# A Hymba-style layer on one Trainium2 core: the second feed-forward's operand blocks moved by 384 bytes, and the ends of its down projections multiplied in token halves

## The chip, the core and the metric

The program runs on one core of one Trainium2 chip. The core has a matrix engine (TensorE, "PE" in the profile, with its weight loads listed apart as "PEld"), a vector engine (DVE), a scalar engine (ACT), GpSimd (POOL) and a queue engine (SP) that issues the loads from HBM. A time is the device time of one launch in microseconds (us). Three runs of the kernel before gave 1117.93, 1118.01 and 1118.09 us. The profile is one more execution, looked at instruction by instruction.

## The reference

One layer over 512 latent tokens and 256 context tokens of width 1024, float32. All three stages run over the latent tokens, and the first two also over the context. The change touches the third stage alone:

```python
def swiglu(h, w1, w3, w2):
    return (jax.nn.silu(h @ w1) * (h @ w3)) @ w2

def ffn_sublayer(h_in, shift, scale, gate, norm_w, w1, w3, w2):
    h = modulate(rms_norm(h_in, norm_w), shift, scale)
    return h_in + 0.5 * gate * swiglu(h, w1, w3, w2)
...
    x = ffn_sublayer(x, mx[0], mx[1], mx[2], norm1_w, ffn1_w1, ffn1_w3, ffn1_w2)
...
    x = x + mx[5] * token_mix(proj, k_all, v_all, rope, q_a_norm_w, w_uq, q_norm_w,
                              v_norm_w, w_s, b_s, w_out)
...
    x = ffn_sublayer(x, mx[6], mx[7], mx[8], norm3_w, ffn2_w1, ffn2_w3, ffn2_w2)
```

With 512 tokens, `w1` and `w3` are 1024 x 2816 and `w2` is 2816 x 1024. The hidden width of 2816 is 22 tiles of 128 columns.

## The kernel before, in words

**Products in three parts.** Activations lie transposed: 128 features on the partitions, tokens along the free axis. Every float32 operand is kept as two tiles, a rounded part (`h`) and the rest (`l`). `mm3` (line 165) makes a product of three matmuls: weights-high with tokens-high, weights-high with tokens-low, weights-low with tokens-high. In the profile's names, `one<-t1h,oph` is a matmul that streams tile `t1h` (the tokens, the moving operand) through the loaded weights `oph` into PSUM bank `one`. Each matmul has its own weight load of 128 x 128.

**The split weights.** Raw weights come from HBM in tiles `raw` or `block`. ACT rounds 512 columns of them into `oph`, and DVE writes the remainder into `opl` (`Stream.split`). There are five such pairs (`OPS = 5`), used in turn.

**The second feed-forward.** Its tokens come as four blocks of 4 feature tiles x 256 tokens: `B11`, `B21` (first 256 tokens), `B12`, `B22` (last 256). The first four hidden tiles (`NPLAIN2 = 4`) are multiplied plainly, 256 tokens at a time (`plain_mm`, lines 168 to 170 in the profile where the scheduler sets the order); part of them take weights from tiles `w0`, `w1` and from the places of `T3` and `T4`. The other 18 hidden tiles go through a Strassen-Winograd scheme (`class Winograd`): seven products each instead of eight, with the blocks `B11`, `B21`, `B22` and the sums `T1` to `T4`. Such a product (`prod`) is 4 feature tiles x 3 matmuls of 128 weights x 256 tokens, so a hidden tile takes 7 x 12 = 84 matmuls. GpSimd and DVE make the sums of weight blocks, ACT and DVE split them and evacuate the banks.

**The down projections.** The 22 hidden tiles are multiplied with `w2` in six chunks, `CHUNKS2 = [4, 4, 4, 4, 2, 4]`. After the last hidden tile of a chunk, `down_flow` (line 746) runs over the 8 output tiles; for each it adds up `n` hidden tiles with `n` x 3 matmuls of 128 weights x 512 tokens into one bank `mm`. Its moving operands are `gh` and `gl`, and its weights are again `oph` and `opl`. The first five chunks take this way (called from `after2`, line 2059); the sixth goes through `down`, at the very end, whose last output tile is done in two halves of 256 tokens.

**What sets the order.** From the Winograd part's start to the fifth down projection the order on every engine is the order written (`nc.ordered = "all"`; all these instructions carry line 59, which is the helper that pins them). What follows is ordered by the scheduler. Line numbers are those of the kernel before.

**Where the tiles lie.** Tiles are taken from pools that grow from both ends of the on-chip memory (SBUF). A tile's start in its partition, in bytes, modulo 512, in the built program:

```
tiles                                       before   after
oph, opl (split weights, all five pairs)       384     384
gh, gl (second feed-forward)                   384     384
B12                                            384     384
B11, B21, B22, T1, T2, T3, T4 (each h and l)   448      64
w0, w1 (each h and l), hfA, squares, rstd      448      64
pth, ptl (attention, moving)                   128     128
vv (attention values, weights)                 448     448
```

Slices of 128 weights and of 256 tokens start at multiples of 512 bytes behind these. "Distance" below is the moving operand's start minus the weights' start, modulo 512: 64 for a block with `oph` or `opl` before (448 - 384), 0 for `gh` or `gl` with `oph` or `opl`, 192 for `pth` with `vv` (128 - 448 + 512).

Of the kernel before, what the change touches and what calls it, by code (L numbers as in the profile page):

```python
# [9 lines left out]
F32 = mybir.dt.float32  # L10
# [7 lines left out]
P = 128  # L18
D = 1024
NK = D // P  # L20
# [11 lines left out]
CHUNKS2 = [4, 4, 4, 4, 2, 4]  # L32
# [132 lines left out]
def mm3(nc, out, lhs, rhs, first, last, more=False):  # L165
    lh, ll = lhs
    rh, rl = rhs
    nc.tensor.matmul(out, lh, rh, start=first, stop=False, skip_group_check=more)  # L168
    nc.tensor.matmul(out, lh, rl, start=False, stop=False, skip_group_check=more)  # L169
    nc.tensor.matmul(out, ll, rh, start=False, stop=last, skip_group_check=more)  # L170
# [3 lines left out]
def layer_kernel(ctx: ExitStack, tc: tile.TileContext, xT, wfirst, wst, wada, wuq, wkpe, cols, wrope, vnw, rope, out):  # L174
    nc = Core(tc)
# [24 lines left out]
    def mm():  # L200
        return ps.tile([P, 512], F32, tag="mm", bufs=4, name=f"mm_{nc.next_id()}")
# [10 lines left out]
    pairs = [[const.tile([P, NK, 2], F32, name=f"{n}{i}") for n in "sag"] for i in range(3)]  # L212
# [189 lines left out]
    def evac_lat(pt, dt, i):  # L402
        nc.vector.scalar_tensor_tensor(lat(x, dt), two(pt), mod_g[i][0][:, dt : dt + 1], lat(x, dt), ALU.mult, ALU.add)
# [286 lines left out]
    def span(t, g, n):  # L690
        if g == "lat":
            return two(t)[:, :, 0:256]
        if g == "ctx":
            return two(t)[:, :, 256:384]
        return t[:, g : g + n]
# [47 lines left out]
        for p in range(2 * n):  # L743
            flow.todo.append(lambda p=p: want(p))

    def down_flow(flow, f0, n, groups, evac, step=lambda dt: None):
        pairs, gone = [], 0
        for dt in range(NK):
            flow.slot(lambda: step(dt))
            while 4 * len(pairs) < dt * n + n:  # L750
                pairs.append(flow.take())
            pts = []
            for g, gn in groups:
                pts.append(mm())
                for fi in range(n):
                    q, o = divmod(dt * n + fi, 4)
                    c = slice(o * P, o * P + P)
                    gh, gl = gt[f0 + fi]
                    mm3(nc, pts[-1][:, :gn], [t[:, c] for t in pairs[q]], (span(gh, g, gn), span(gl, g, gn)), fi == 0, fi == n - 1)
            for (g, gn), pt in zip(groups[:-1], pts):  # L760
                evac(pt, dt, g, gn)
            def last(pt=pts[-1], dt=dt, g=groups[-1]):
                evac(pt, dt, *g)
                yield

            flow.pend = [last()]
            flow.spent = (dt * n + n) // 4 - gone
            gone += flow.spent

    starts1 = [sum(CHUNKS1[:i]) for i in range(len(CHUNKS1))]  # L770
    starts2 = [sum(CHUNKS2[:i]) for i in range(len(CHUNKS2))]
# [203 lines left out]
    def after1(flow, f):  # L975
        for ci in ends1(f):
            down_flow(flow, starts1[ci], CHUNKS1[ci], [GA, GB], lambda pt, dt, g, gn: evac_x(pt, dt, seg_of(g // 384), 0),
                      lambda dt: ada_step(2))
# [61 lines left out]
    flow = Flow(OPS)  # L1040
# [35 lines left out]
    for f in range(NFIRST, NPLAIN1):  # L1076
# [7 lines left out]
        for w in range(2):  # L1084
            pair = None
            for g in (1, 0) if last else (0, 1):
# [12 lines left out]
                for k in range(NK):  # L1099
                    c = slice(k % 4 * P, k % 4 * P + P)  # L1100
# [5 lines left out]
                if w == 1:  # L1106
# [3 lines left out]
                    def evac(f=f, pb=(pb[g, 0], pb[g, 1]), c=slice(384 * g, 384 * g + 384)):  # L1110
                        gh, gl = gt[f]
                        sl = gp.tile([P, 384], F32, tag="sl", bufs=1, name=f"sl_{nc.next_id()}")
                        nc.scalar.activation(sl, pb[0][:, :384], AF.Silu)
                        nc.vector.tensor_mul(sl, pb[1][:, :384], sl)
                        yield
                        g_split(sl, gh[:, c], gl[:, c])
# [57 lines left out]
    def last_mm(g, dt):  # L1174
        pt = mm()
        c = slice(384 * g, 384 * g + 384)
        for fi in range(lastn):
            q, o = divmod(dt * lastn + fi, 4)
            gh, gl = gt[lastf + fi]
            mm3(nc, pt[:, :384], [t[:, o * P : o * P + P] for t in lastp[q]], (gh[:, c], gl[:, c]), fi == 0, fi == lastn - 1)  # L1180
        return pt
# [35 lines left out]
    pt = None  # L1217
    for dt in range(NK):
# [5 lines left out]
        pt = last_mm(0, dt)  # L1224
# [4 lines left out]
    def in_want(i, w):  # L1229
        if w == 0:  # L1230
            inw[i].append(st.half(wst, U_IN + i))
        src = inw[i][0][:, w * 512 : w * 512 + 512]
        inw[i].append(homes[2] if i == 2 and w else st.pair())
        hi, lo = inw[i][-1]
        nc.scalar.copy(hi, src)
        return lambda: nc.vector.tensor_sub(lo, src, hi.bitcast(F32))

    TILES = (0, 1, 2, 1, 2, 1, 1, 0)
    for dt in range(NK):
        w = in_want(dt - 5, 0) if dt > 4 else None  # L1240
# [10 lines left out]
        pt = last_mm(1, dt)  # L1251
# [367 lines left out]
    heads, pes, pts, sms, ols = {}, {}, {}, {}, {}  # L1619
# [231 lines left out]
    with right():  # L1851
        hap = hactx.enter_context(tc.tile_pool(name="hap", bufs=1))

    def block(pool, name):
        return tuple(pool.tile([P, 4, 256], F32R, bufs=1, name=f"{name}{p}") for p in "hl")

    B11, B21 = block(hap, "b11"), block(hap, "b21")
    hbctx = ExitStack()
    with right():
        hbp = hbctx.enter_context(tc.tile_pool(name="hbp", bufs=1))  # L1860
# [134 lines left out]
    def ends2(f):  # L1995
        return [ci for ci in range(len(CHUNKS2) - 1) if starts2[ci] + CHUNKS2[ci] == f]
# [33 lines left out]
    flow = Flow(OPS)  # L2030
# [27 lines left out]

    def after2(flow, f):
        for ci in ends2(f):  # L2060
            down_flow(flow, starts2[ci], CHUNKS2[ci], [(0, 512)], lambda pt, dt, g, gn: evac_lat(pt, dt, 2))

    nc.ordered = "all"
    wino.run(flow, NPLAIN2, after2, splits=splits)
    nc.ordered = False
    lastu = {}
# [104 lines left out]
```

## Time and profile before

| what | value |
|---|---|
| median of three runs | 1118.01 us |
| the profiled execution's own time | 1118.25 us |
| its span, first to last instruction | 1116.5 us |
| granted TensorE clock over the span | 1.000 |
| matmuls / weight loads | 7208 / 7208 |
| DVE, ACT, POOL busy | 80%, 48%, 28% of the span |
| last down projection's start to the end of the span | from about 1088 us to 1116.5 us |

A matmul's duration in the profile is modelled and longer than the time after which the next one starts, since matmuls are pipelined. What a matmul costs is the distance between two starts. So the views of use are the timeline (start times of single instructions), and windows laid exactly around a stretch of equal matmuls, whose length divided by their number is the cost of one.

### The profile page before, as it was taken

To read this page: it belongs to the slowest core of one execution; us is meant where nothing else is said; L and a number is where in the kernel's file an instruction comes from. 1 tells how busy PE (TensorE), PEld (TensorE's weight loads), DVE (VectorE), ACT (ScalarE), POOL (GpSimd) and SP (SyncE) were. 2 spreads that over 40 slices of the span, in tenths; PEclk is the share of its full clock that TensorE was granted. 3 is DMA by queue.
4 is the path that set the end of the run, shared out by engine and by line. 5 is a ranking of instruction groups with operands and counts; after the bars stand their busy time and mean duration, and the time that the engine had idled before them with its cause. 6 is when DMAs were issued, how large, how long until landed. Compare 5 with 4: busy or idle time off the path is not lost.

```text
span 1116.5 us, 18983 instructions
## 1 busy us (share of the span) xinstructions
PE 1111.0 (100%) x7208; PEld 1062.8 (95%) x7208; DVE 888.9 (80%) x1638; ACT 538.6 (48%) x1110; POOL 310.8 (28%) x268
## 2 busy tenths in 40 slices
PE   9999999999999999999999999999999999999998
PEld 7899999999999999999988889999999989898997
DVE  5779898888888789867756899978887869686884
ACT  6545412431444214444745559985554535353451
POOL 0002303312233023300018427750014435161330
PEclk9999999999999999999999999999999999999999
DMA  9721353344333665322243111003121422233302
GB/s 359 266 69 45 131 163 123 113 137 147 124 114 143 235 196 187 116 63 74 86 148 95 60 38 40 20 20 123 68 97 59 149 75 104 90 110 113 114 1 95
DMA packets 35675, 125.91 MB, mean 113 GB/s; under 512 B 3712, under 2 KB 10624, under 8 KB 30976
## 3 DMA queue, kind: packets, MB, share of 16 engines
q1 hardware_dynamic: 35440, 124.63, 32.9%
q8 instruction: 57, 0.93, 0.3%
q14 instruction: 34, 0.28, 0.1%
q10 hardware_dynamic: 144, 0.06, 0.0%
HBM read 122.58 MB, written 2.10 MB: 112 GB/s over the span
## 4 chain that ended last, share of the span: by engine, by line
PE 96%; DMA 1%; DVE 1%; ACT 1%; issue 0%; POOL 0%; SPq 0%; ACTq 0%; DVEq 0%; POOLq 0%
PE mm L59 57%; PE one L59 20%; PE big L59 8%; PE mm L168 2%; PE mm L169 2%; PE mm L170 2%; PE big L595 1%; PE mm L580 1%; DMA scale<-wada 1%; PE big L170 1%; PE big L168 1%; PE big L169 1%; PE mm L329 1%; DMA x<-xT 0%; PE big L587 0%; DVE sq L59 0%
## 5 line engine op out<-in xcount | busy, mean ns | idle before, releaser
L59 DVE TENSOR_TENSOR opl<-block,oph 128x512 fp32r<-128x512 f32 x216 | 192.1, 896 | 29.0 <-ACT oph L59 26.4
L59 POOL TENSOR_TENSOR block<-block 128x512 f32<-128x512 f32 x69 | 105.0, 1521 | 382.2 <-DVE opl L59 379.5
L59 ACT CAST oph<-block 128x512 fp32r<-128x512 f32 x216 | 133.8, 621 | 112.0 <-PE mm L59 85.1
L59 PE MATMUL mm<-gh,oph 128*128 128x384 f32 (+1 forms) x440 | 155.4, 353 | 0.0
L59 PE MATMUL mm<-gh,opl 128*128 128x384 f32 (+1 forms) x440 | 155.0, 352 | 0.0
L59 PE MATMUL mm<-gl,oph 128*128 128x384 f32 (+1 forms) x440 | 154.9, 352 | 0.0
L59 DVE SCALAR_TENSOR_TENSOR x<-mm,g,x 128x256 f32<-128x256 f32 (+2 forms) x184 | 84.6, 498 | 46.8 <-PE mm L59 46.7
L59 ACT CAST oph<-raw 128x512 fp32r<-128x512 f32 x113 | 68.6, 620 | 78.5 <-PE mm L59 52.9
L59 PEld LDWEIGHTS mm<-gh,opl 128*128 128x128 f32 x440 | 82.6, 188 | 5.7
L59 PEld LDWEIGHTS mm<-gl,oph 128*128 128x128 f32 x440 | 82.6, 188 | 5.6
L59 PEld LDWEIGHTS mm<-gh,oph 128*128 128x128 f32 x440 | 82.6, 188 | 5.6
L59 DVE TENSOR_TENSOR opl<-raw,oph 128x512 fp32r<-128x512 f32 x113 | 77.7, 702 | 9.8 <-ACT oph L59 9.1
L59 POOL TENSOR_TENSOR block<-s,block 128x512 f32<-128x512 f32 x35 | 47.8, 1366 | 131.9 <-DVE opl L59 131.0
L59 PE MATMUL mm<-hh,oph 128*128 128x384 f32 x192 | 64.9, 338 | 0.0
L59 PE MATMUL mm<-hh,opl 128*128 128x384 f32 x192 | 64.5, 336 | 0.0
L59 PE MATMUL mm<-hl,oph 128*128 128x384 f32 x192 | 64.5, 336 | 0.0
L59 DVE SCALAR_TENSOR_TENSOR junk<-raw,cb 128x1024 bf16<-128x1024 f32 x48 | 62.2, 1309 | 0.0
L59 POOL TENSOR_TENSOR s<-block 128x512 f32<-128x512 f32 x34 | 55.8, 1641 | 9.4 <-DMA block<-wst 9.4
L59 PE MATMUL one<-hh,opl 128*128 128x384 f32 x144 | 48.4, 336 | 0.0
L59 PE MATMUL one<-hh,oph 128*128 128x384 f32 x144 | 48.4, 336 | 0.0
L59 PE MATMUL one<-hl,oph 128*128 128x384 f32 x144 | 48.4, 336 | 0.0
L59 DVE SCALAR_TENSOR_TENSOR raw<-raw,cb 128x1024 f32<-128x1024 f32 x32 | 41.0, 1288 | 8.4 <-DMA raw<-wada 8.3
(711 smaller groups left out, 3386.1 us busy)
## 6 DMA issues: line engine op xcount, KB each, us to landing
raw<-wst SPq DMA_DIRECT2D x77, 512.0 KB, 3.8
block<-wst SPq DMA_DIRECT2D x36, 1024.0 KB, 5.0
raw<-wada SPq DMA_DIRECT2D x56, 512.0 KB, 4.1
scale<-wada SPq DMA_DIRECT2D x16, 512.0 KB, 9.1
x<-xT SPq DMA_DIRECT2D x5, 512.0 KB, 6.5
raw<-wfirst SPq DMA_DIRECT2D x8, 256.0 KB, 8.9
out<-x SPq DMA_DIRECT2D x7, 256.0 KB, 2.2
raw<-wuq SPq DMA_DIRECT2D x2, 384.0 KB, 5.0
```

The source lines that it names most:

```text
L59: return lambda *a, **k: self.tc.keep_in_program_order(f(*a, **k))
L168: nc.tensor.matmul(out, lh, rh, start=first, stop=False, skip_group_check=more)
L169: nc.tensor.matmul(out, lh, rl, start=False, stop=False, skip_group_check=more)
L170: nc.tensor.matmul(out, ll, rh, start=False, stop=last, skip_group_check=more)
L329: pin(nc.tensor.matmul(pa[q, :P], scw[:, kt, 2 - 2 * w : 34 - 2 * w], units[d][w][:, kt * P : kt * P + P], start=w == 0 and kt < 4, stop=w ...
L580: pin(nc.tensor.matmul(o, l[:, c], r, start=k == 0 and m == 0 and w == 0, stop=k == NK - 1 and m == 2, skip_group_check=True))
L595: pin(nc.tensor.matmul(two(pbs[i]), ops[k][lo][:, i * P : i * P + P], lat(r, k), start=False, stop=k == NK - 1 and m == 2, skip_group_chec ...
```

## The change

Three edits. A tile of 96 float32 (384 bytes) that nothing uses is taken from the pool `hap` behind `B11` and `B21`; by it the tiles listed above as 64 start 384 bytes lower. `down_flow` gets a switch `halved`: with it, in the last output tile (`dt == NK - 1`) the last two hidden tiles (for a chunk of two, only the last, since the first must open the bank's sum over all 512 tokens) are multiplied with 256 tokens and then with the other 256, three matmuls each. The second feed-forward's five `down_flow` calls set it.

```diff
-    def down_flow(flow, f0, n, groups, evac, step=lambda dt: None):
+    def down_flow(flow, f0, n, groups, evac, step=lambda dt: None, halved=False):
...
                     gh, gl = gt[f0 + fi]
-                    mm3(nc, pts[-1][:, :gn], [t[:, c] for t in pairs[q]], (span(gh, g, gn), span(gl, g, gn)), fi == 0, fi == n - 1)
+                    w = gn // 2 if halved and dt == NK - 1 and fi >= max(n - 2, 1) else gn
+                    for o in range(0, gn, w):
+                        mm3(nc, pts[-1][:, o : o + w], [t[:, c] for t in pairs[q]], (span(gh, g + o, w), span(gl, g + o, w)),
+                            fi == 0, fi == n - 1 and o + w == gn)
...
     B11, B21 = block(hap, "b11"), block(hap, "b21")
+    hap.tile([P, 96], F32, name="pad_hap")
...
-            down_flow(flow, starts2[ci], CHUNKS2[ci], [(0, 512)], lambda pt, dt, g, gn: evac_lat(pt, dt, 2))
+            down_flow(flow, starts2[ci], CHUNKS2[ci], [(0, 512)], lambda pt, dt, g, gn: evac_lat(pt, dt, 2), halved=True)
```

On DVE, ACT, POOL and SP the same instructions stand in the same order as before. On PE the order differs at the five ends of down projections alone. The first of them, before (a `gh`/`gl` pair is one hidden tile; `one<-t1h` begins the next hidden tile's products):

```order
L59 MATMUL mm_10405<-gl_9611,oph_10314 128x512
L59 MATMUL mm_10405<-gh_9609,opl_10316 128x512
L59 MATMUL mm_10405<-gh_9630,oph_10314 128x512
L59 MATMUL mm_10405<-gl_9632,oph_10314 128x512
L59 MATMUL mm_10405<-gh_9630,opl_10316 128x512
L59 MATMUL mm_10405<-gh_9998,oph_10314 128x512
L59 MATMUL mm_10405<-gl_10000,oph_10314 128x512
L59 MATMUL mm_10405<-gh_9998,opl_10316 128x512
L59 MATMUL one_10169<-t1h,oph_10335 128x256
```

The same place in the changed kernel (buffer numbers are one higher):

```order
L59 MATMUL mm_10406<-gh_9631,opl_10317 128x256
L59 MATMUL mm_10406<-gh_9999,oph_10315 128x256
L59 MATMUL mm_10406<-gl_10001,oph_10315 128x256
L59 MATMUL mm_10406<-gh_9999,opl_10317 128x256
L59 MATMUL mm_10406<-gh_9999,oph_10315 128x256
L59 MATMUL mm_10406<-gl_10001,oph_10315 128x256
L59 MATMUL mm_10406<-gh_9999,opl_10317 128x256
L59 MATMUL one_10170<-t1h,oph_10336 128x256
```

Six matmuls of 512 tokens have become twelve of 256 at four ends, and three have become six at the end of the chunk of two: 27 fewer of the one kind and 54 of the other.

## The prediction

> **What bounds the kernel now.** I read the page's busy times and its chain of waits first, to see which engine sets the end.
>
> ```profile
> span 1116.5 us, 18983 instructions
> PE 1111.0 (100%) x7208; PEld 1062.8 (95%) x7208; DVE 888.9 (80%) x1638; ACT 538.6 (48%) x1110; POOL 310.8 (28%) x268
> PE 96%; DMA 1%; DVE 1%; ACT 1%; issue 0%; POOL 0%; SPq 0%; ACTq 0%; DVEq 0%; POOLq 0%
> ```
>
> The chain that ended last lies on PE for 96% of the span. PE is never idle for long, so the time is the number of matmuls times the time from one start to the next. Second, windows cut at the first matmul of each stretch of the second feed-forward: five Winograd stretches between down projections, the first one before them, and two down projections to compare. The columns are the stretch, its length, then busy us and instructions of PE, PEld, DVE, ACT and POOL.
>
> ```profile
> 813.64:826.36 12.72, 12.72 (x110) 12.72 (x109) 11.70 (x24) 8.13 (x19) 0.00 (x0) 1.00 0.31 103
> 848.16:887.73 39.57, 39.57 (x337) 39.57 (x336) 35.12 (x57) 22.60 (x49) 19.83 (x13) 1.00 0.30 102
> 887.73:909.53 21.80, 21.80 (x98) 18.02 (x97) 12.47 (x20) 5.92 (x12) 4.16 (x3) 1.00 0.32 106
> 909.53:949.11 39.58, 39.58 (x338) 39.58 (x337) 35.13 (x57) 22.52 (x49) 19.82 (x13) 1.00 0.29 102
> 970.90:1010.48 39.58, 39.58 (x337) 39.57 (x336) 35.12 (x57) 22.53 (x49) 19.84 (x13) 1.00 0.30 102
> 1032.28:1052.07 19.79, 19.79 (x170) 19.79 (x169) 16.69 (x28) 11.07 (x24) 7.22 (x5) 1.00 0.31 106
> 1062.98:1088.43 25.45, 25.45 (x218) 25.44 (x217) 21.80 (x37) 14.46 (x31) 8.51 (x6) 1.00 0.01 2
> ```
>
> The counts include one or two matmuls still in flight at an edge. By the program, 4 hidden tiles x 84 = 336 matmuls start in each long stretch, 168 and 216 in the two shorter ones, 108 in the first. The six lengths add up to 176.69 us for 1500 matmuls: **117.8 ns** each, and every stretch alone gives the same (39.57 / 336 = 117.8, 12.72 / 108 = 117.8). PE is busy through all of it and the clock column says 1.00, so this is a pace, not a wait. Third, I looked in the timeline for other matmuls of 128 weights x 256 tokens at other distances between moving tile and weights. Each pair of rows below is the first and the last of a run; the columns are start and duration.
>
> ```profile
> 744.75 0.28 PE L59 MATMUL mm<-ptl,vv 128*128 128x256 f32 x1
> 746.00 0.28 PE L59 MATMUL mm<-pth,vv 128*128 128x256 f32 x1
> ...
> 781.47 0.28 PE L59 MATMUL big<-b11h,oph 128*128 128x256 f32 x1
> 786.80 0.28 PE L59 MATMUL big<-b21h,opl 128*128 128x256 f32 x1
> ...
> 1110.55 0.28 PE L170 MATMUL mm<-gh,opl 128*128 128x256 f32 x1
> 1113.07 0.28 PE L170 MATMUL mm<-gh,opl 128*128 128x256 f32 x1
> ```
>
> Distance 0 (`gh` with `opl`, the last output tile): 22 matmuls, 2.52 us / 21 = **120.0 ns**. Distance 192 (`pth` or `ptl` with `vv`): 12 matmuls, 1.25 us / 11 = **113.6 ns**. Distance 64 has two paces: 117.8 in the Winograd stretches, but 5.33 us / 47 = **113.4 ns** over the 48 matmuls of one plain product. So the shape alone does not set the pace. The distance has to do with it, and at 64 something else decides between two paces: how the run is entered, I think. The entries show that.
>
> ```profile
> 781.35 0.28 PE L59 MATMUL mm<-b21h,t4l 128*128 128x256 f32 x1
> 781.59 0.28 PE L59 MATMUL big<-b11l,oph 128*128 128x256 f32 x1
> 781.70 0.28 PE L59 MATMUL big<-b11h,opl 128*128 128x256 f32 x1
> ...
> 847.93 0.39 PE L59 MATMUL mm<-gh,opl 128*128 128x512 f32 x1
> 848.16 0.28 PE L59 MATMUL one<-t1h,oph 128*128 128x256 f32 x1
> 848.75 0.28 PE L59 MATMUL one<-t1h,opl 128*128 128x256 f32 x1
> ```
>
> The quick plain product at 781.47 is entered from 256-token matmuls at distance 0 (both tiles at 448) and is quick from its second matmul on. The Winograd stretch at 848.16 is entered from 512-token matmuls, runs 0.12 per matmul from the start and stays there for 336. Both halves of the change fit this picture: the pad moves the blocks to distance 192, and the halves make the entry one from 256-token matmuls.
>
> **The change part by part.** *The pad.* It moves no instruction. The 1500 Winograd matmuls go from distance 64 to 192. The nearest row for a block at 192 is the attention run above. It is short, so I looked at how its kind begins elsewhere, after matmuls of 384 columns:
>
> ```profile
> 694.11 0.34 PE L59 MATMUL big<-kth,qtl 96*128 96x384 f32 x1
> 694.29 0.28 PE L59 MATMUL mm<-pth,vv 128*128 128x256 f32 x1
> 694.41 0.28 PE L59 MATMUL mm<-ptl,vv 128*128 128x256 f32 x1
> 694.52 0.28 PE L59 MATMUL mm<-pth,vv 128*128 128x256 f32 x1
> 694.64 0.28 PE L59 MATMUL mm<-ptl,vv 128*128 128x256 f32 x1
> 694.86 0.28 PE L59 MATMUL mm<-ptl,vv 128*128 128x256 f32 x1
> ```
>
> The first takes 0.12, the next ones 0.11 to 0.12, the last two 0.11 each: at 192 a run that begins at 120 falls to about 113.5 within four matmuls, and does not stay at 117.8 as at 64. Bounds for the new pace: from below 113.3, since no run of 256 tokens here keeps a lower one; from above 120.0, the highest steady one. I take 113.4, the pace of that plain product, which is within a quarter of a nanosecond of the one at 192. So 1500 x (117.8 - 113.4) = **6.6 us less**, between 6.75 less and 3.3 more. Each of the six entries may cost its first matmuls some 10 ns over the pace, as at 694.29: 0.06 in all.
>
> The plain products change a little. `B22` with split weights goes from 64 to 192; these are 48 matmuls.
>
> ```profile
> L168 PE MATMUL mm<-b22h,oph 128*128 128x256 f32 x8 | 2.2, 281 | 0.0
> L168 PE MATMUL mm<-b12h,t3h 128*128 128x256 f32 x4 | 1.1, 281 | 0.0
> L168 PE MATMUL mm<-b21h,oph 128*128 128x256 f32 x8 | 2.2, 276 | 0.0
> ```
>
> Modelled durations move with the pace (`B21`, in the product at 113.4, has 276). 48 x (281 - 276) bounds the gain by 0.24; I take 0.15. `B12` with `w0`, `w1`, `T3`, `T4` goes from 448 to 320, which no run here shows; 48 matmuls of 276 to 284 by the rows around them give 0.4 either way at most, and I take nothing. `B11` and `B21` keep distance 0 to `w0`, `w1`, `T3` and `T4`, since all of these move together, and their products with split weights are already at the fast pace.
>
> *The halves.* 27 matmuls of 512 tokens become 54 of 256, all at distance 0. A 512-token matmul takes (1110.32 - 1109.64) / 3 = 226.7 ns, a half 120.0 by the run at 1110.55:
>
> ```profile
> 1109.64 0.39 PE L168 MATMUL mm<-gh,oph 128*128 128x512 f32 x1
> 1110.32 0.28 PE L168 MATMUL mm<-gh,oph 128*128 128x256 f32 x1
> ```
>
> 27 x (240.0 - 226.7) = **0.36 us more**, on PE and so on the path. The 27 further weight loads lie under the streaming of the matmul before, as all others do. The switch from 512 to 256 at distance 0 shows nothing beyond that: 1110.32 to 1110.55 is 0.23 for two.
>
> *Who feeds PE.* If PE is faster by 1.5 us in a long stretch (336 x 4.4 ns), DVE must keep up: 35.12 busy of then 38.1, 92%; in the first stretch 11.70 of 12.24, 96%. The view of waits over these stretches has no row for PE. Two of its three largest kinds are these (total us, times, longest), and below them stands the window of the plain product at 781.47:
>
> ```profile
> POOL block L59 <- DVE opl L59: 154.1, 27, 20.1
> ACT oph L59 <- PE mm L59: 67.9, 43, 2.1
> 781.35:786.90 5.55, 5.55 (x51) 5.55 (x50) 4.98 (x12) 3.36 (x8) 0.00 (x0) 1.00 0.43 147
> ```
>
> ACT waits 67.9 us for PE to give back a pair of weights: the splitting runs ahead and is held back by PE. The down projections between, with DVE busy 12.47 of 21.80, let it refill the five pairs. And the run at 781.47 kept its pace with DVE busy 4.98 of 5.55, 90%. So I take no stall; if the cover is gone, it costs at most what the stretch gained.
>
> *The sum.* Against the profiled execution's 1118.25 (its span of 1116.5 and 1.75 around it): -6.6 - 0.15 + 0.06 + 0.36 = -6.33, or 1111.9. The median of the runs is 0.24 below the profiled one: **1111.7**.
>
> [...]
>
> **The rivals.** *One: the pace hangs on the entry alone, and the distance does nothing.* For it: both paces exist at 64. The halves would then have to make the good entry, and another entry from 256 tokens at distance 0 failed:
>
> ```profile
> 810.66 0.28 PE L170 MATMUL mm<-b12h,opl 128*128 128x256 f32 x1
> 810.78 0.28 PE L168 MATMUL mm<-b22h,oph 128*128 128x256 f32 x1
> 811.01 0.28 PE L170 MATMUL mm<-b22h,opl 128*128 128x256 f32 x1
> 811.37 0.28 PE L170 MATMUL mm<-b22h,opl 128*128 128x256 f32 x1
> ```
>
> From `B12` at distance 0 into `B22` at 64 the run goes on at 0.12 (0.36 for three), not at 113.4. If the new entries fail like this, 1500 matmuls stay at 117.8 and only the halves remain: 1118.01 + 0.36 = 1118.4. Against it: the runs with `vv`, which come down to 113.5 from a start at 120.
>
> *Two: part of the gain.* The first stretch has no halves before it, and DVE has only half a microsecond to spare there; stretches could settle between the paces, or the splitting could stop PE late in a long one, where 1.5 us of lead are used up. Half of the gain: 1118.0 - 3.3 + 0.4 = 1115.1. For it: 96% for DVE. Against it: no wait of PE at all before.
>
> *Three: slower.* The halves are at distance 0, the slowest pace there is, and they stand right before the blocks. If a run keeps the pace with which it is entered, as the one at 848.16 keeps its own for 336 matmuls, the Winograd stretches take 120.0: 1392 x 2.2 = 3.1 more, and 0.36 for the halves, 1121.5. It decides once the pace in the blocks is above 117.8 - 0.36 / 1.5 = 117.6 ns. Against it: at 781.47 a run left that pace with its second matmul.
>
> *Four: the change does not do what it says*, for instance because the pad is left out of the layout. It is in: the built program's blocks start at 64 modulo 512. I give it nothing.
>
> **How the numbers follow.** The forecast gets 0.70: both a distance that showed 113.6 and an entry that led to 113.4 once. Rival one gets 0.09, two 0.14, three 0.07. The forecast's own range is 1111.0 to 1112.8 (the pace from 113.3 to 113.9, the plain products' 0.4 either way). To leave out no more than 2 in 10 it needs a part of the cases of half a gain: 1110.9 to 1115.2. Below 1110.9 nothing in the trace leads. A measurement of this kernel can tell 0.2%, 2.2 us, from no change: the forecast and nearly all of two are faster by more (0.83), one is the same (0.10), three is slower (0.07).
>
> **What would show it.** In the profile after, the windows of the Winograd stretches are 38.1 (336 matmuls), 19.1 (168) and 24.5 (216) if the pace is 113.4, and the first is 12.2. A down projection's last six 512-token matmuls show as twelve, 120 ns apart, and its window is 0.08 longer. The chain stays on PE. Wrong would be: windows that still divide to 117.8 (rival one), new rows of PE waiting for DVE or for ACT (two), 120 in the blocks (three), or 113.4 behind the halves only, with the first stretch at 117.8, which would say that the entry counts and the distance little.

## The result, and the profile after

The changed kernel takes 1114.64 us (median of 8 runs, 1114.45 to 1115.15), the kernel before 1117.95 us in runs on the same chip. The ratio is 0.9971, 95% interval 0.996 to 0.9981. That is 3.3 us less where 6.3 were forecast, with about half of the gain missing. It lies inside the stated range (1110.9 to 1115.2), but outside the forecast's own (1111.0 to 1112.8), and near the 1115.1 of rival two.

The page of the changed kernel begins with the span and the busy times, and its chain stays on PE:

```profile
span 1113.2 us, 19037 instructions
PE 1106.1 (99%) x7235; PEld 1058.1 (95%) x7235; DVE 887.8 (80%) x1638; ACT 537.7 (48%) x1110; POOL 308.4 (28%) x268
PE 95%; DVE 2%; DMA 1%; ACT 1%; issue 0%; POOL 0%; SPq 0%; ACTq 0%; DVEq 0%; POOLq 0%
```

PE fell from 100% to 99%, and DVE stands on the chain with 2% where it had 1%. PE now stops somewhere. The windows of the same six Winograd stretches and of one down projection between them, with the columns as in the prediction:

```profile
814.10:826.36 12.26, 12.26 (x110) 12.26 (x109) 11.16 (x23) 7.60 (x18) 0.00 (x0) 1.00 0.30 105
848.21:887.17 38.96, 38.68 (x338) 38.28 (x337) 34.84 (x56) 22.45 (x49) 19.65 (x13) 1.00 0.29 100
887.17:909.02 21.85, 21.85 (x105) 18.33 (x103) 12.68 (x21) 5.79 (x11) 4.16 (x3) 1.00 0.32 113
909.02:948.01 38.99, 38.70 (x338) 38.31 (x337) 34.85 (x56) 22.42 (x49) 19.66 (x13) 1.00 0.30 100
969.84:1008.83 38.99, 38.71 (x339) 38.32 (x337) 34.84 (x56) 22.44 (x49) 19.64 (x13) 1.00 0.29 100
1030.70:1049.76 19.06, 19.06 (x170) 19.06 (x169) 16.25 (x27) 10.88 (x23) 7.19 (x5) 1.00 0.30 99
1060.69:1085.19 24.50, 24.50 (x219) 24.50 (x217) 21.20 (x37) 14.36 (x31) 8.50 (x6) 1.00 0.01 2
```

Three stretches are what was forecast (12.2, 19.1, 24.5): 24.50 / 216 = 113.4 ns. The three long ones are not 38.1 but 38.96 to 38.99, and in them alone PE's busy time is below the length, by 0.28 or 0.29 us. The view of waits over all stretches, which had no row for PE before, has one now, and PEld has two (total us, times, longest):

```profile
PE mm L59 <- DVE u L59: 0.8, 3, 0.3
PEld mm L59 <- DVE u L59: 1.4, 3, 0.5
PEld one L59 <- DVE u L59: 0.6, 3, 0.2
```

The timeline of PE shows one of the six stops, in the third tile of the first long stretch:

```profile
875.20 0.28 PE L59 MATMUL one<-t4l,oph 128*128 128x256 f32 x1
875.32 0.28 PE L59 MATMUL one<-t4h,opl 128*128 128x256 f32 x1
875.60 0.38 PE L59 MATMUL one<-b22h,oph 128*128 128x256 f32 x1
875.82 0.28 PE L59 MATMUL one<-b22l,oph 128*128 128x256 f32 x1
```

From 875.32 to 875.82 pass 0.50 us for two starts that take 0.23 elsewhere: 0.27 lost, just ahead of the product with `B22`. The same place in the fourth tile (885.13 to 885.68 for one start) loses the rest of the 0.86 (38.96 - 38.10). Outside these stops the long stretches run at the forecast pace as well. Here is what DVE does until then, and after it POOL (start, duration):

```profile
867.38 0.98 DVE L59 TENSOR_TENSOR opl<-block,oph 128x512 fp32r<-128x512 f32 x1
...
868.62 1.44 DVE L59 TENSOR_TENSOR opl<-block,oph 128x512 fp32r<-128x512 f32 x1
...
873.66 0.41 DVE L59 TENSOR_TENSOR u<-one,p 128x256 f32<-128x256 f32 x1
873.99 0.68 DVE L59 TENSOR_TENSOR opl<-s,oph 128x512 fp32r<-128x512 f32 x1
874.59 0.42 DVE L59 TENSOR_TENSOR one<-one,u 128x256 f32<-128x256 f32 x1
875.12 0.42 DVE L59 TENSOR_TENSOR u<-one,u 128x256 f32<-128x256 f32 x1
```

```profile
866.20 1.61 POOL L59 TENSOR_TENSOR block<-block 128x512 f32<-128x512 f32 x1 [3.90 <-DVE opl L59]
867.77 1.74 POOL L59 TENSOR_TENSOR s<-block 128x512 f32<-128x512 f32 x1
```

`u<-one,u` at 875.12 is the last read of bank `one` (`u3 = Z + u3`) before the product with `B22` adds to that bank. It ends at 875.54 and PE starts at 875.60. In the first two tiles the same read ends 1.69 and 0.45 us before that product starts, so the margin is used up along the stretch. DVE takes its instructions in the order written, and has little room between them (34.84 us busy of 38.96). The split into `opl` takes 0.68 us alone (873.99), but 0.98 and 1.44 beside a block sum of POOL: the first ends at 868.36, 0.55 after POOL's 866.20 + 1.61, the second at 870.06, 0.55 after POOL's 867.77 + 1.74. It is the same along the whole stretch. All eleven splits that begin while a sum runs end 0.55 or 0.56 after that sum and last 0.69 to 1.78 us; the sixteen others take 0.67 to 0.69. So a split that begins beside a sum seems to wait for it and to do most of its work behind it.

### The profile page after: what moved, and what is told of

It is laid out like the page before. It is cut to its first block, busy times and chain, and to the rows that moved or that the text cites. A ratio compares the mean times of both kernels' runs of the same rounds, so it can differ in the third digit from the quotient of the medians.

```text
span 1113.2 us, 19037 instructions
## 1 busy us (share of the span) xinstructions
PE 1106.1 (99%) x7235; PEld 1058.1 (95%) x7235; DVE 887.8 (80%) x1638; ACT 537.7 (48%) x1110; POOL 308.4 (28%) x268
## 4 chain that ended last, share of the span: by engine, by line
PE 95%; DVE 2%; DMA 1%; ACT 1%; issue 0%; POOL 0%; SPq 0%; ACTq 0%; DVEq 0%; POOLq 0%
PE mm L59 56%; PE one L59 19%; PE big L59 8%; PE mm L169 2%; PE mm L168 2%; PE mm L170 2%; PE big L595 1%; PE mm L580 1%; DMA scale<-wada 1%; PE big L168 1%; PE big L170 1%; PE big L169 1%; PE mm L329 1%; DMA x<-xT 1%; DVE opl L59 0%; ACT oph L59 0%
## 5 line engine op out<-in xcount | busy, mean ns | idle before, releaser
L59 PE MATMUL mm<-gh,oph 128*128 128x384 f32 (+2 forms) x449 | 156.9, 349 | 0.0
L59 PE MATMUL mm<-gl,oph 128*128 128x384 f32 (+2 forms) x449 | 156.6, 349 | 0.0
L59 PE MATMUL mm<-gh,opl 128*128 128x384 f32 (+2 forms) x449 | 156.6, 349 | 0.0
```

What stands on the lines that cost most here:

```text
L59: return lambda *a, **k: self.tc.keep_in_program_order(f(*a, **k))
```

## The experiments

**Each half of the change alone.** The first kernel has the pad without the halves, the second the halves without the pad.

```diff
-            down_flow(..., lambda pt, dt, g, gn: evac_lat(pt, dt, 2), halved=True)
+            down_flow(..., lambda pt, dt, g, gn: evac_lat(pt, dt, 2))
```

> The changed kernel without the halves: down projections end with 512-token matmuls as before, blocks at distance 192. If the distance alone sets the pace, every Winograd stretch still runs at 113.3 ns per matmul and the time is that of the changed kernel less the 0.36 us of the halves, about 1114.3. If the entry decides, the five stretches behind a down projection go back to 117.8 (39.57 us for the long ones), only the first stretch keeps 113.5, and the time is about 1118.0. If each does part, single stretches differ.

```diff
-    hap.tile([P, 96], F32, name="pad_hap")
```

> The changed kernel without the pad: blocks at distance 64 again, down projections end in halves. If the entry alone sets the pace, the five stretches behind a down projection run at 113.3 ns as in the changed kernel, and since the plain products keep their 113.4 the time is about 1114.2 to 1114.7. If the distance is needed, they stay at 117.8 (39.57 us) and only the price of the halves remains: 1118.3.

With the pad alone: 1117.92 us, ratio 0.9989 to 1.0008. With the halves alone: 1118.40 us, 0.9994 to 1.0013. Neither brings anything to the total. The first long stretch with the pad alone:

```profile
847.96:887.53 39.57, 39.57 (x337) 39.57 (x336) 35.10 (x57) 22.66 (x49) 19.80 (x13) 1.00 0.30 102
```

With the halves alone:

```profile
848.03:887.61 39.58, 39.58 (x338) 39.58 (x337) 35.13 (x57) 22.66 (x49) 19.84 (x13) 1.00 0.30 101
```

Both divide to 117.8 ns, as before. With the pad alone that stretch starts like this:

```profile
847.73 0.39 PE L59 MATMUL mm<-gh,opl 128*128 128x512 f32 x1
847.96 0.28 PE L59 MATMUL one<-t1h,oph 128*128 128x256 f32 x1
...
849.37 0.28 PE L59 MATMUL one<-b21h,oph 128*128 128x256 f32 x1
```

The first twelve take 1.41 us, 117.5 each: at distance 192, entered from a down projection that ends with 512 tokens, the run does not come down. In these five stretches the quick pace needs the distance and the halves together. The first stretch, which is entered from `B12` in every kernel, has the quick pace with the pad alone as well: it lasts from 813.93 to 826.18, 12.25 us where it took 12.72. The plain products before it, slower with the pad, take most of that back.

**Which load makes DVE late.** The next two kernels take work from DVE ahead of the late read. One leaves the multiplication of W with the silu values (`tensor_mul(W, W, sl)`) out of the second feed-forward's Winograd tiles, 0.43 us a tile. The other moves the subtraction for `gl` of the second 256 tokens one slot later.

```diff
-                v.tensor_mul(W, W, sl)
+                if self.held is None:
+                    v.tensor_mul(W, W, sl)
```

> The changed kernel with one vector operation less for each hidden tile of the second feed-forward's Winograd part: the product of the first 256 tokens with the silu (about 0.42 us) is left out. If VectorE's work is what stops PE in the three long stretches, it has 1.7 us less to do in each, the two stops in each (about 0.3 and 0.55 us) are gone, the long stretches take 38.1 us, and the time falls by 2.6 us to about 1112.0. If the stops come from something else (a bank not free, ScalarE, GpSimd), they stay and the time is 1114.6.

```diff
...
-                g_split(Z, gh[:, n:], gl[:, n:])
+                if self.held is None or f + 1 == NF:
+                    g_split(Z, gh[:, n:], gl[:, n:])
+                    return
+                nc.scalar.copy(gh[:, n:], Z)
+
+                def rest():
+                    yield
+                    v.tensor_sub(gl[:, n:], Z, gh[:, n:].bitcast(F32))
+
+                self.flow.late.append(rest())
```

> The changed kernel with one vector operation moved, nothing left out: the remainder gl of the second 256 tokens is made one slot later, behind the next weight split, so that VectorE does not wait for ScalarE's gh in front of it (0.44 us for each hidden tile). If VectorE's time is what stops PE in the long stretches, 1.3 us of waiting in each go, more than the 0.87 us of stops, and the time falls by up to 2.6 us, to about 1112.0 to 1112.6. If the stops come from something else, 1114.6.

Without the multiplication: 1114.67 us, ratio 0.9958 to 0.998, the same as the changed kernel. The first long stretch:

```profile
847.86:886.85 38.99, 38.96 (x339) 38.63 (x337) 34.97 (x54) 22.52 (x49) 19.68 (x13) 1.00 0.30 100
```

DVE has three multiplications fewer in the window than in the changed kernel and one split more (54 instructions against 56), and is as long busy (34.97 against 34.84). The split behind the missing instruction starts earlier, waits for the same block sum, and ends no earlier: the 21 splits of `block` in the window take 22.2 us, 20.8 in the changed kernel. So at this place the number of DVE's instructions doesn't set when it is through; what they wait for does. PE shows it too. The third tile's stop is as long as before (874.97 to 875.27). The run behind it then takes 117.8 ns a start (60 starts from 876.79 to 883.86), but the stretch is no longer for it: the fourth tile's stop is shorter instead (885.15 to 885.36 for one start), because the read that it waits for comes when it came before.

With `gl` moved: 1117.12 us, 0.9983 to 1.0001, 2.5 us more than the changed kernel, where a gain was expected. DVE no longer waits 0.44 us for ACT's `gh`, but 0.96 for ACT's `oph` ahead of the next split, so the late read comes 0.5 us later in the stretch than in the changed kernel. The stops are longer:

```profile
873.90 0.28 PE L59 MATMUL one<-t4l,oph 128*128 128x256 f32 x1
...
875.03 0.28 PE L59 MATMUL one<-t4h,opl 128*128 128x256 f32 x1
875.80 0.38 PE L59 MATMUL one<-b22h,oph 128*128 128x256 f32 x1 [0.49 <-DVE u L59]
...
884.26 0.28 PE L59 MATMUL one<-b11h,opl 128*128 128x256 f32 x1
```

The rows show something else besides. From 875.80 to 884.26 lie 71 starts (six products of twelve, less one): 8.46 us; the first step takes 0.22 (to 876.02 in the same view), and the other 70 divide to 117.7 ns. The ten starts ahead of the stop take 1.13, 113 each. The stop itself was a new entry, and a bad one. The second long stretch shows the same. In the third one the run behind an equal stop kept its pace (60 starts from 1000.58 to 1007.38, 113.3 each), and in the changed kernel the stops, at the same product, didn't change it either. The stop's length does not decide this: in the kernel without the multiplication 0.30 us between two starts was followed by 117.8.

**GpSimd's part.** Here three of the four block sums of a tile in the second feed-forward's Winograd part are left out, so most products there get other weights (the first tile of the first long stretch, whose sums are made during the down projection ahead of it, loses only one); the splits stay.

```diff
+                if self.held is not None and f != self.held:
+                    return
...
-                eng[0].tensor_sub(q[1], q[1], q[0])
+                if self.held is None:
+                    eng[0].tensor_sub(q[1], q[1], q[0])
```

> The changed kernel without three of GpSimd's four sums of weight blocks for each hidden tile of the second feed-forward's Winograd part (the weights are then not the sums that the scheme needs; splits, products and evacuations stay). The trace of the changed kernel shows VectorE's weight splits at 0.68 us alone and up to 1.78 us where a GpSimd sum runs beside them. If this stretching is why VectorE is late with the sum that PE waits for in the third and fourth tile of a long stretch, every split takes about 0.7 us, the stops of PE are gone, the long stretches take 38.1 us, and the time falls by 2.6 us to about 1112.0. If VectorE is late for another reason, the stops stay and the time is 1114.6.

1111.99 us, ratio 0.9932 to 0.996, and no wait of PE is left. The first long stretch:

```profile
847.77:885.87 38.10, 38.10 (x339) 38.10 (x337) 30.98 (x58) 22.87 (x50) 4.54 (x3) 1.00 0.34 118
```

This is the forecast's 38.1. DVE has as much to do (58 instructions in the window, 56 in the changed kernel) and is busy 30.98 us, not 34.84. The difference lies in the splits of `block`. These are their rows for the first long stretch of the changed kernel, of the one without the multiplication, and of this one (number, busy us, mean ns):

```profile
L59 DVE TENSOR_TENSOR opl<-block,oph 128x512 fp32r<-128x512 f32 x21 | 20.8, 1005 | 2.0 <-ACT oph L59 1.6
L59 DVE TENSOR_TENSOR opl<-block,oph 128x512 fp32r<-128x512 f32 x21 | 22.2, 1073 | 2.0 <-ACT oph L59 1.6
L59 DVE TENSOR_TENSOR opl<-block,oph 128x512 fp32r<-128x512 f32 x21 | 15.9, 757 | 4.2 <-ACT oph L59 3.5
```

POOL's ten further sums stretch the same 21 splits by 4.9 us. And what three multiplications of 0.43 saved, the splits used up by waiting 1.4 us more.

One of the sums could go to DVE instead. The next kernel gives it one of the four.

```diff
-                eng[0].tensor_sub(q[1], q[1], q[0])
+                (eng[0] if self.held is None else nc.vector).tensor_sub(q[1], q[1], q[0])
```

> The changed kernel with one of the four sums of weight blocks for each hidden tile made by VectorE instead of GpSimd (about 0.7 us more for VectorE, 1.6 us less for GpSimd), nothing left out. If a split held up by GpSimd costs VectorE more than that, the stops of PE in the long stretches shrink and the time is 1112.0 to 1114; if VectorE's own work counts, it is late by 2.8 us more in each long stretch and the time is above 1116.

1123.49 us, ratio 1.0035 to 1.0066: slower than before. The waits of PE over the stretches:

```profile
PE mm L59 <- DVE u L59: 5.8, 7, 0.9
PE one L59 <- DVE u L59: 2.4, 3, 0.9
```

In the first long stretch DVE's splits together take no less than in the changed kernel (25.5 us against 24.9): those of `block` take 18.5, but those of `s`, which took 0.68 each alone, now stand beside POOL's remaining sums and take 1.45. The three sums in the window (2.1 us) come on top. DVE has no room for one sum a tile.

**Another order on DVE.** At the slot of the late read, the kernel starts a split (`opl<-s` at 873.99 above) ahead of it. The next kernel holds that split back until the read is through, in the last two tiles of each long stretch.

```diff
-        self.fill()
+        if not hold:
+            self.fill()
...
-                self.product(banks[3], "T3", True, ev_u3())
+                self.product(banks[3], "T3", True, ev_u3(), hold=self.held is not None and f in (7, 8, 11, 12, 15, 16))
```

> The changed kernel with VectorE's order altered in the third and fourth tile of each long stretch, nothing left out: the weight split in front of u3 (the sum that PE's last product of a tile waits for) comes behind it. By the theory that VectorE is merely late there with a sum that PE needs now, while the split has 0.9 us or more to spare, each of the six stops (0.3 and 0.55 us) shrinks by about 0.7 us: the time falls by 2 to 2.6 us to about 1112.0 to 1112.6. If the split is needed as soon, PE stops for the weights instead and the time is 1114.6 or more.

1113.59 us (1113.36 to 1113.9), ratio 0.9948 to 0.9973. DVE at the place of the first stop:

```profile
874.74 0.42 DVE L59 TENSOR_TENSOR u<-one,u 128x256 f32<-128x256 f32 x1
875.08 0.68 DVE L59 TENSOR_TENSOR opl<-s,oph 128x512 fp32r<-128x512 f32 x1
```

The read now starts at 874.74 (with everything 0.10 later than in the changed kernel) and the third tile's stop is gone. The long stretches take 38.60, 38.60 and 38.59 us: the fourth tile still stops, by 0.5. Its read ends 0.35 us earlier in the stretch than in the changed kernel, but PE, without the third tile's stop, is there 0.30 earlier. So the gain is 1.1 us, where 2 to 2.6 were expected.

**Other distances.** Three pads put the blocks elsewhere: 80 floats at 256 bytes past the split weights, 112 floats at 128, the latter with the halves and without them. A fourth kernel adds the hold to the pad of 112 with the halves.

```diff
-    hap.tile([P, 96], F32, name="pad_hap")
+    hap.tile([P, 80], F32, name="pad_hap")
```

> The changed kernel with a pad of 320 bytes: blocks at distance 256 from the split weights, halves kept. If the distance alone sorts the paces with 192 in a middle of good ones, the Winograd stretches run at 113.3 as at 192; if 192 is a narrow place, they run at 117.8 or 120 and the time is 1118 to 1122.

```diff
-    hap.tile([P, 96], F32, name="pad_hap")
+    hap.tile([P, 112], F32, name="pad_hap")
```

> The changed kernel with a pad of 448 bytes: blocks at distance 128 from the split weights, halves kept. At 256 the pace was 120.0 like at 0, so the pattern may repeat every 256 bytes, and 128 would be the farthest from 0. If so, every run of block products reaches 113.3 whatever precedes it, the plain products with B11 and B21 too: the long stretches keep VectorE's stops, and the time is 1114.6 less 0.4, about 1114.2. If 128 is like 64 (117.8 after every entry), 1118.4.

> Blocks at distance 128 and no halves. If at 128 the pace no longer depends on the entry, the stretches behind 512-token matmuls run at 113.3 too and the time is about 1113.9 (1114.2 less the halves' 0.36). If the entry still decides, they run at 117.8 and the time is about 1117.5 to 1118.0.

> Distance 128, halves, and VectorE's altered order of the run after_hold. If 128 only adds the plain products to what after_hold had (1113.6), the time is about 1113.1. If 128 is worse than 192, it is above 1113.6.

At 256: 1122.68 us in the one run. At 128 with the halves: 1120.39, ratio 1.0012 to 1.003; without them: 1122.10, 1.0023 to 1.005; with the hold: 1120.39, 1.0012 to 1.003. The first long stretch of the kernel at 256:

```profile
849.21:889.52 40.31, 40.31 (x338) 40.31 (x337) 35.38 (x58) 22.60 (x50) 19.38 (x13) 1.00 0.30 102
```

At 128 with the halves:

```profile
848.75:888.63 39.88, 39.88 (x339) 39.88 (x337) 35.23 (x58) 22.74 (x49) 19.83 (x13) 1.00 0.30 104
```

At 128 without them:

```profile
849.06:889.38 40.32, 40.32 (x337) 40.31 (x336) 35.39 (x58) 22.58 (x50) 19.40 (x13) 1.00 0.31 104
```

Divided by 336, with the paces measured above:

| distance | behind a down projection with halves | behind one that ends with 512 tokens |
|---|---|---|
| 64 | 117.8 ns | 117.8 ns |
| 128 | 118.7 ns | 120.0 ns |
| 192 | 113.4 ns | 117.8 ns |
| 256 | 120.0 ns | not tried |

The pads move the blocks and leave the split weights where they are, so the table does not tell the distance from the blocks' own place. At distance 0 the place made no difference: `B21` with `T3` and `T4`, both at 448 before and both at 64 after, takes 2.51 us for 21 starts in either kernel (from 778.96 and from 779.00), 119.5 each, and `gh` with `oph`, both at 384, takes 120.

The hold changes nothing at 128, since PE is never stopped there (busy 39.88 of 39.88 us): at 118.7 ns DVE has the time that it lacks at 113.4.

**Shorter stretches.** The last kernel keeps pad, halves and hold, and cuts the twelve tiles of the three long stretches into four stretches of three, with one group of down projections more between them. The lines taken out are those of the kernel with the hold.

```diff
-CHUNKS2 = [4, 4, 4, 4, 2, 4]
+CHUNKS2 = [4, 3, 3, 3, 3, 2, 4]
...
-                self.product(banks[3], "T3", True, ev_u3(), hold=self.held is not None and f in (7, 8, 11, 12, 15, 16))
+                self.product(banks[3], "T3", True, ev_u3(), hold=self.held is not None and f in (7, 10, 13, 16))
```

> The changed kernel with both edits kept, the early weight split held back behind u3 as in after_hold, and the twelve middle tiles of the second feed-forward cut into four stretches of three in place of three of four. If VectorE's lateness builds up over a stretch (stops of 0.3 us before the third tile and 0.5 us before the fourth in the changed kernel), no stretch lives long enough to stop TensorE: the three remaining stops of after_hold, 3 x 0.49 us, go, one more entry at the slow pace and one more group of down projections cost about 0.1 us, and the time is about 1112.2 us. If the lateness does not depend on the length of the stretch, or the fourth group of down evacuations (eight more of 0.75 us each on VectorE) takes the cover away, stops of TensorE for VectorE's u stand in the stretches of three as well and the time is 1113.6 us or more.

1112.35 us (1112.25 to 1112.43), ratio 0.9934 to 0.9962 to the kernel before. Three of its four stretches of 252 matmuls are alike; the second is a little longer:

```profile
847.94:876.52 28.58, 28.58 (x255) 28.58 (x253) 25.10 (x41) 16.61 (x36) 13.42 (x9) 1.00 0.28 95
892.92:921.68 28.76, 28.76 (x254) 28.74 (x253) 24.93 (x40) 16.66 (x36) 13.42 (x9) 1.00 0.27 90
```

28.58 / 252 = 113.4 ns, and the view of waits over the stretches has no row for PE. DVE's lateness builds up over a stretch, and with the hold three tiles are too few for it to reach PE: the read in the third tile ends 0.36 us before the product starts, in the longer second stretch only 0.08. Without the hold the changed kernel stopped in the third tile already; three tiles without it were not tried. This is the fastest version that leaves nothing out, 5.8 us under the kernel before and 2.3 under the changed one's median.

## Why the prediction was right, and where it was not

The working was made against the profiled execution, which went from 1118.25 to 1114.98 us: 3.27 less, where the sum said 6.33.

| term | forecast | measured |
|---|---|---|
| 1500 Winograd matmuls, with their entries | -6.54 | 176.69 to 172.76: -3.93 |
| plain products before them | -0.15 | 813.64 to 814.10: +0.46 |
| halves in five groups of down projections | +0.36 | +0.23 (0.02 to 0.07 each; 21.80 to 21.85 in the one quoted) |

The three make -3.24; 0.03 lies behind the last stretch.

**The pace** was right: without the stops the six stretches take 172.76 - 2.64 = 170.12 us, 113.4 ns each, and the entries are within 0.1 us of nothing. The doubt about the first stretch, which has no halves ahead of it, was unfounded (12.26 us). That the pad and the halves are both needed, the two kernels with one of them alone show. Rival one, the entry alone, is out: with the halves and the old distance the stretches stay at 117.8, with the halves and 192 they run at 113.4. The reason given for the pad, that a run at 192 comes down to 113.5 by itself as after 384 columns, was too wide. By it the pad alone would have done, and behind 512-token down projections it stays at 117.8. The prediction held here because the change had the halves too. The paces at 128 and 256 also take away the trend that 120.0, 117.8 and 113.6 at 0, 64 and 192 suggested: a distance of 256 is as slow as 0.

**The failed step is "So I take no stall".** It costs 38.96 + 38.99 + 38.99 - 3 x 38.10 = 2.64 us, which is 2.6 of the missing 3.1. The prediction came near it in rival two ("the splitting could stop PE late in a long one"), with a time of 1115.1, and gave that 0.14. That this time is so close is luck: half of the gain was taken there, not worked out. The measured time is inside the stated range only because the range had been drawn out for that rival. What misled was the evidence for the cover. ACT waiting 67.9 us for pairs of weights shows that the splitting runs ahead, and it did. But PE doesn't stop for split weights: it stops for DVE's read of a bank, which stands behind those splits in the order written (the read at 875.12, a split at 873.99). And DVE's 92% of a long stretch were read as a load that stays; a good part of them is DVE's waiting for GpSimd's sums, as the kernel without three of them shows (30.98 us in place of 34.84). The margin could be read in the profile before. There the fourth tile's read of the first long stretch and the product that needs its bank are these:

```profile
885.52 0.42 DVE L59 TENSOR_TENSOR u<-mm,u 128x256 f32<-128x256 f32 x1
886.32 0.28 PE L59 MATMUL mm<-b22h,oph 128*128 128x256 f32 x1
```

The read ends 0.38 us ahead (0.60 in the third tile, 0.92 in the second), while the forecast pace brings PE there 1.4 us earlier (324 starts of 4.4 ns less; 1.1 in the third tile). The plain product with DVE 90% busy, quoted as proof of cover, has POOL at 0.00 in that very row.

**Plain products.** That those of `B11` and `B21` with split weights keep their pace, as "already at the fast pace", was wrong. The first of them, 48 matmuls from the first row to the second:

```profile
781.51 0.28 PE L59 MATMUL big<-b11h,oph 128*128 128x256 f32 x1
...
787.16 0.28 PE L168 MATMUL big<-b12h,oph 128*128 128x256 f32 x1
```

5.65 / 48 = 117.7 ns, 113.4 before, so 0.21 us more. The second one shows the same in its modelled duration (276 before):

```profile
L168 PE MATMUL mm<-b21h,oph 128*128 128x256 f32 x8 | 2.2, 281 | 0.0
```

Two such products are 0.42 of the 0.46. They went to distance 192 with the other blocks, but their entry, from `B21` or `B22` with `t4`, moved along with both its tiles, and from there 192 is slow and 64 was quick. The prediction priced their old entry as if the distance had not changed. The rest is small: the two passages with `B22` and split weights gain 0.04 and 0.07, where 0.15 were taken, and `B12` with `w0` and `w1` loses 0.09, where nothing was. Twelve of the 48 matmuls of `B22` in that term also stand in the first stretch's 108, so the sum counted them twice (0.05).

**The halves** cost 0.23, not 0.36. In the window quoted they cost 0.05, where 6 x 13.3 ns = 0.08 were forecast: the step was the right one and mis-sized by a third, since the run's first steps are shorter than 120 and the whole takes 119 each. Its rows in the first group:

```profile
846.78 0.28 PE L59 MATMUL mm<-gh,oph 128*128 128x256 f32 x1
846.89 0.28 PE L59 MATMUL mm<-gl,oph 128*128 128x256 f32 x1
...
848.21 0.29 PE L59 MATMUL one<-t1h,oph 128*128 128x256 f32 x1
```

The first start is followed after 0.11, and the twelve take 1.43 us, 119 each.

**Still open** is why the pace hangs on the entry. At 192 the quick pace comes from halves at distance 0, from 384 columns, and in the first stretch from `B12`; it doesn't come from a whole down projection of 512 tokens, nor from `B21` with `t4`, and a stop of PE can end it (the kernel with `gl` moved) or leave it (the changed kernel). Nor is an entry from 512 tokens slow in itself. Behind the last stretch a product with `T4` follows two 512-token matmuls; in the changed kernel its twelve take 1.37 us, 114 each:

```profile
1085.65 0.28 PE L59 MATMUL one<-t4h,oph 128*128 128x256 f32 x1
1087.02 0.39 PE L168 MATMUL mm<-gh,oph 128*128 128x512 f32 x1
```

With the pad alone, at the same distance and behind the same two matmuls, they take 1.41 (from 1088.52), 117.5 each; in the kernel before, at 64, 1.36 (from 1088.89), 113 each. So what ran ahead of the two counts as well. No run here separates what these entries have in common. No price for an untried distance follows from the table either.

## What to carry to other kernels

When PE is made faster by some per cent, look for every engine's instruction that PE waits for through a bank, not only for the one that feeds it weights. Read in the trace before how long ahead of PE it ends, and compare that with how much earlier PE will come. List what stands ahead of it in the order written, with durations as they are beside the other engines' work (here 1.44 us for a split that takes 0.68 alone). A busy share can include waiting that another engine causes (here 34.84 us with GpSimd's sums, 30.98 without three of four): take that engine's work out of one run before calling the share load. A pace measured at one operand distance and one entry was not that of another pair (at 192, 113.4 ns behind the halves and 117.8 behind 512 tokens); each pair has to be measured in its place.

## What the runs showed of the hardware that was not expected

- One shape of matmul (128 x 128 weights, 256 tokens) has steady paces of 113.4, 117.8, 118.7 and 120.0 ns, at the distances tried, 0 to 256 bytes modulo 512, and behind the entries met here. A run can keep its pace for 336 matmuls (39.57 us before, 38.10 with three block sums left out).
- From distance 64 to 192, the pad and the entry brought their gain behind the down projections only together: 0.12 us less for the pad alone (1117.92 against 1118.04) and 0.36 more for the halves alone, but 6.0 us less for both when PE isn't stopped (1118.00 to 1111.99, with three block sums left out).
- Taking three multiplications off VectorE in a stretch freed nothing (34.97 us busy against 34.84), and taking ten sums off GpSimd freed 3.9 us of VectorE.
- A stop of PE can set the pace of the run behind it anew, and its length doesn't decide how. 0.30 us between two starts was followed by 117.8 ns (without the multiplication), 0.28 left 113.4 (the changed kernel), and with a sum on DVE a stop in which PE was idle for 0.57 us moved a run from 117.7 back to 113.3 (60 starts from 931.23 to 938.29, and 60 from 941.92 to 948.72).
